# Gate and up of the half steps by a block algorithm with seven products for eight, with the output product in thirds and a list-scheduled order

## The chip, the cores and the metric

The kernel runs on one core of a Trainium2 chip. The time is the device time of one execution in microseconds; lower is better. The engines are TensorE (PE: matmuls, with its weight loads shown apart as PEld), VectorE (DVE), ScalarE (ACT), GpSimd (POOL) and SyncE (SP, which issues the DMAs here).

## What is computed

A decoder trunk of two layers on 512 tokens of width 1024 in float32. Each layer is a half step, a mixer and a second half step; the change is in the four half steps:

```python
def swiglu(x, wi, wo):
    gate, up = jnp.split(x @ wi, 2, axis=-1)
    return (jax.nn.silu(gate) * up) @ wo
...
        h = h + 0.5 * swiglu(rms_norm(h, ffn1_norm[li]), ffn1_wi[li], ffn1_wo[li])
        hn = rms_norm(h, mix_norm[li])
...
        h = h + mix
        h = h + 0.5 * swiglu(rms_norm(h, ffn2_norm[li]), ffn2_wi[li], ffn2_wo[li])
```

`wi` is 1024 x 5632 (gate and up, 2816 features each), `wo` is 2816 x 1024. The mixer of layer 0 is gated linear attention beside causal pooling (`gla_pool_mixer`), that of layer 1 sparse attention with an indexer that chooses 128 keys (`dsa_mixer`); a final norm ends the trunk.

## The kernel before

All activations lie transposed in SBUF: `h` is eight tiles of 128 features x 512 tokens. A float32 product is made of three passes of PE: every operand is kept as a high and a low part (`hi` + `lo`), and `mm3` (L152 to L156) issues high x high, high x low, low x high. The high part is a ScalarE copy to float32r, the low part a VectorE subtraction. `post` (L215) makes these parts of `h` times the norm's gain, `hgh0..7` and `hgl0..7`. The norm's factor `R` (one number per token) is multiplied in afterwards.

Weights come as chunks of 128 x 2048 in the order of their use. `w_load` issues the DMA into one of two raw tiles `wr`, `w_split` (L121) makes `wh` (L144) and `wl` (L145) of the whole chunk and then loads the chunk after the next; `w_get` hands out the parts. Each of `wr`, `wh` and `wl` has two buffers.

A half step, `ffn` (L250), goes through the 22 feature blocks in two halves of 11. For a block it runs 8 tiles x gate and up x 3 passes = 48 matmuls of 512 columns into two PSUM banks. `evac` (L253) makes the activation: gate times `R` (L255), silu (L256), up times `R` (L258), their product (L259), high part `acth` (L262) and low part `actl` (L263). After eleven blocks the output product adds 8 tiles `m` of 11 blocks, each 33 matmuls of 512 columns into one bank (`out_block`, L308), and L327 adds half the bank to `h[m]`. In the second half of a half step `post` and `squares` prepare the next norm. The last half step makes its two last output tiles in pieces of 256 tokens, so that the norm and the stores of the first 256 lie beside the products of the second (`piece`, `final`).

Instructions go to each engine in the order in which the program calls them, written out by hand: `w_split` and `bg_step` after each block (the latter runs steps of the rotary tables in the second half step). Engines wait on each other through semaphores. The mixers use the same stream of weights: `proj` (L377) for projections of 512 columns, `v_mm` (L535) and `v_tile` for values, with the weights as the moving operand on 256 columns, `eo_pool` (L793) and `oo` (L1080) for their output products.

SBUF tiles are laid out pool after pool and, inside a pool, in order of first use, each padded to a multiple of 32 bytes; pools stand in the order `const`, `wpool`, `hgpool`, `small`, then the pool of the stage at hand.

## Time and profile before

| | us |
|---|---|
| median of 3 runs | 1850.26 |
| lowest, highest | 1849.87, 1858.63 |
| span of the profiled execution | 1855.0 |
| busy in it: PE, PEld, VectorE, ScalarE, GpSimd | 1834.0, 1494.0, 887.9, 599.6, 195.7 |

The span runs from the first to the last instruction of the one profiled execution. A matmul's listed duration overlaps the next one's, so the step from one start to the next is what it costs; the busy time of PE is the union of all of them. A row's last part, in brackets or behind a bar, is the idle time of the engine before it and what ended it.

### The profile page before, as it was taken

What the parts mean: (1) busy time and instruction counts of PE and PEld (TensorE: products, weight loads), DVE (VectorE), ACT (ScalarE), POOL (GpSimd) and SP (SyncE); (2) the same over time, 40 slices, a digit from 0 to 9 for tenths busy, and PEclk for the clock granted to TensorE, in tenths of its full rate; (3) what the DMA queues carried; (4) which work ended last, traced back from release to release, by engine and by line L of the source; (5) the groups of instructions that cost most, each with busy time, mean ns of one, the idle gap of its engine ahead of it and who ended that gap; (6) DMA issues with size and microseconds to landing.
All of it is one profiled execution on the core that took longest, in us unless ns stands there. A gap on an engine that the chain in (4) does not pass through costs nothing.

```text
span 1855.0 us, 19748 instructions
## 1 busy us (share of the span) xinstructions
PE 1834.0 (99%) x8330; PEld 1494.0 (81%) x8330; DVE 887.9 (48%) x1144; ACT 599.6 (32%) x717; POOL 195.7 (11%) x159
## 2 busy tenths in 40 slices
PE   9999999999999999999999999999999999999997
PEld 6888888888678888888888888888687888888886
DVE  6442444348455552444344424444797444334443
ACT  5321223243253322223333212233346432212232
POOL 0000000134320000000100000001475200000002
PEclk9999999999899999999999999999999999999999
DMA  5222222131112232222232222222121122222221
GB/s 184 91 102 91 93 111 92 62 126 69 46 69 97 93 111 81 101 104 91 79 114 91 101 93 91 98 107 82 60 92 46 69 91 99 105 99 93 92 91 57
DMA packets 28361, 169.97 MB, mean 92 GB/s; under 512 B 3152, under 2 KB 6128, under 8 KB 9072
## 3 DMA queue, kind: packets, MB, share of 16 engines
q1 hardware_dynamic: 28272, 168.71, 25.0%
q8 instruction: 65, 1.06, 0.2%
q14 instruction: 24, 0.20, 0.0%
HBM read 166.60 MB, written 2.10 MB: 91 GB/s over the span
## 4 chain that ended last, share of the span: by engine, by line
PE 92%; DVE 4%; issue 1%; ACT 1%; POOL 1%; DMA 0%; SPq 0%; DVEq 0%; ACTq 0%; POOLq 0%
PE o L155 9%; PE o L154 9%; PE o L156 9%; PE g L156 9%; PE u L156 9%; PE u L154 9%; PE u L155 9%; PE g L154 9%; PE g L155 9%; PE pj L154 2%; PE pj L155 1%; PE pj L156 1%; PE oo L155 1%; PE oo L154 1%; PE oo L156 1%
## 5 line engine op out<-in xcount | busy, mean ns | idle before, releaser
L145 DVE TENSOR_TENSOR wl<-wr,wh 128x2048 fp32r<-128x2048 f32 (+3 forms) x151 | 323.6, 2144 | 299.5 <-ACT wh L144 298.8
L144 ACT ACTIVATE wh<-wr 128x2048 fp32r<-128x2048 f32 (+3 forms) x166 | 298.1, 1797 | 249.1 <-PE o L155 179.7
L154 PE MATMUL o<-acth,wh 128*128 128x512 f32 (+1 forms) x726 | 281.3, 387 | 0.0
L155 PE MATMUL o<-actl,wh 128*128 128x512 f32 (+1 forms) x726 | 281.1, 387 | 0.0
L156 PE MATMUL o<-acth,wl 128*128 128x512 f32 (+1 forms) x726 | 281.1, 387 | 0.0
L154 PE MATMUL g<-hgh_f,wh 128*128 128x512 f32 x704 | 275.8, 392 | 1.7 <-ACT wh L144 1.7
L154 PE MATMUL u<-hgh_f,wh 128*128 128x512 f32 x704 | 274.5, 390 | 0.0
L156 PE MATMUL g<-hgh_f,wl 128*128 128x512 f32 x704 | 274.4, 390 | 0.1
L155 PE MATMUL g<-hgl_f,wh 128*128 128x512 f32 x704 | 274.3, 390 | 0.0
L155 PE MATMUL u<-hgl_f,wh 128*128 128x512 f32 x704 | 274.1, 389 | 0.0
L156 PE MATMUL u<-hgh_f,wl 128*128 128x512 f32 x704 | 274.0, 389 | 0.0
L230 POOL TENSOR_TENSOR acc<-acc,sq 128x512 f32<-128x512 f32 x35 | 53.1, 1518 | 1482.7 <-ACT sq L229 1482.7
L258 DVE TENSOR_TENSOR u<-u,R 128x512 f32<-128x512 f32 x88 | 60.7, 690 | 300.6 <-PE u L156 300.6
L262 ACT ACTIVATE acth<-u 128x512 fp32r<-128x512 f32 x88 | 55.6, 632 | 373.2 <-DVE u L259 373.2
L154 PEld LDWEIGHTS o<-acth,wh 128*128 128x128 f32 x726 | 136.0, 187 | 31.6
L155 PEld LDWEIGHTS o<-actl,wh 128*128 128x128 f32 x726 | 135.9, 187 | 31.5
L156 PEld LDWEIGHTS o<-acth,wl 128*128 128x128 f32 x726 | 135.9, 187 | 31.3
L154 PEld LDWEIGHTS g<-hgh_f,wh 128*128 128x128 f32 x704 | 132.2, 188 | 32.1 <-ACT wh L144 4.1
L155 PEld LDWEIGHTS g<-hgl_f,wh 128*128 128x128 f32 x704 | 132.4, 188 | 28.7 <-issue 0.7
L156 PEld LDWEIGHTS g<-hgh_f,wl 128*128 128x128 f32 x704 | 132.2, 188 | 28.0 <-DVE wl L145 0.6
L155 PEld LDWEIGHTS u<-hgl_f,wh 128*128 128x128 f32 x704 | 132.2, 188 | 27.8 <-issue 0.2
L156 PEld LDWEIGHTS u<-hgh_f,wl 128*128 128x128 f32 x704 | 132.3, 188 | 27.6
(286 smaller groups left out, 2070.1 us busy)
## 6 DMA issues: line engine op xcount, KB each, us to landing
wr<-in_wi_dram SPq DMA_DIRECT2D x87, 1024.0 KB, 4.8
wr<-in_wo_dram SPq DMA_DIRECT2D x40, 1024.0 KB, 4.8
wr<-in_wev_dram SPq DMA_DIRECT2D x8, 1024.0 KB, 4.8
wr<-in_wod_dram SPq DMA_DIRECT2D x7, 1024.0 KB, 4.8
wr<-in_wo_dram SPq DMA_DIRECT2D x8, 512.0 KB, 3.7
wr<-in_wevo_dram SPq DMA_DIRECT2D x4, 1024.0 KB, 4.8
wr<-in_wodo_dram SPq DMA_DIRECT2D x4, 1024.0 KB, 4.8
h<-in_xT_dram SPq DMA_DIRECT2D x8, 256.0 KB, 6.2
```

Of the source, the lines that this page charges most:

```text
L144: A.activation(hi[:, p0:p1], raw[:, p0:p1], AF.Copy)
L145: eng.tensor_tensor(lo[:, p0:p1], raw[:, p0:p1], hi[:, p0:p1], op=ALU.subtract)
L154: T.matmul(ps, st[0], mv[0], start=start, stop=False)
L155: T.matmul(ps, st[0], mv[1], start=False, stop=False)
L156: T.matmul(ps, st[1], mv[0], start=False, stop=stop)
L230: (eng or G).tensor_tensor(acc[:, a:b], acc[:, a:b], sq[:, a:b], op=ALU.add)
L258: V.tensor_tensor(u1, up, R, op=ALU.mult)
L262: A.activation(hi, u1, AF.Copy)
```

## The change

Gate and up of feature blocks 3 to 21 are computed by a block algorithm on 2 x 2 blocks: of the weights, gate and up by the first and second half of the 1024 inputs; of the activations, the first and second half of the inputs by the first and second half of the tokens. Seven products of 128 x 512 by 512 x 256 take the place of eight, and sums of blocks are formed before and after them:

- Of each weight chunk (`"S"`, stored as four blocks of 512 columns and loaded by two DMAs) VectorE forms four sums (`outer`, one operation of 1024 columns, and two of 512). `split_part` makes high and low parts of three stretches, `ab` (1024 columns, unit 0), `ds` (1536, unit 2 or 3 in turn) and `z` (1024, unit 1). The units hold the parts in single buffers.
- Of the activations `add_blocks` forms four sums per pair of tiles once in a half step: `TH` and `TL`, in 4 tiles of 1024 columns each.
- `seven_products` runs 7 products of 4 tiles x 3 passes of 256 columns into two banks, `A_` and `BC`. ScalarE copies partial sums out of them (`s1`, `s5`, `s2`, `t4`), VectorE adds (`gate`, `u3`). Products seven and four of a block run between the first products of the next one, or inside the first output tile. Up is no longer multiplied by `R`; the output is (`scaled`, two VectorE operations per tile instead of one).

Blocks 0 to 2 (`PLAIN`) stay as they were. The output product is made after 8, 7 and 7 blocks (`THIRDS`) instead of after 11 and 11, so `h[m]` is added to three times. A half step is first built as a list of tasks with durations and dependences (`Schedule`), and then issued in the order in which a list schedule of these tasks on the engines starts them; PE's order and the DMA queue's are kept as they are written.

Tiles move: `hgpool` stands before `wpool`, small tiles named `shift` are put in, weight units begin at an offset (`off`, in words of 4 bytes) by the kind of use, a 4-byte tile goes out of the pool of the rotary tables, and the scratch space at the bottom shrinks from 16384 to 1024 bytes. Four tiles of the first mixer and six of the second move into the tails of the raw tiles. The last products of the second mixer run as two of 256 columns instead of one of 512. The core of the diff:

```diff
+THIRDS = ((0, 8), (8, 15), (15, 22))
+PLAIN = (0, 1, 2)
+UNIT = 1024
+UPAD = 64
...
+        while any(queues.values()):
+            best = None
+            for eng, q in queues.items():
+                for t in q[:1] if eng in ("PE", "SP") else q:
+                    if all(d.end is not None for d in t.deps):
+                        ready = max([clock[eng]] + [d.end + (self.LAG if d.eng != eng else 0.0) for d in t.deps])
+                        key = (ready, t.late, t.n)
+                        if best is None or key < best[0]:
+                            best = (key, t)
+            (start, _, _), t = best
+            t.end = clock[t.eng] = start + t.dur
+            queues[t.eng].remove(t)
+            done.append(t)
+        for t in done:
+            t.fn()
+        return clock
...
+    def chunk(kind, src, n, eng=V, units=(0, 1), off=0):
+        chunks.append((kind, src, n, eng, units, off))
     def ffn_chunks(i):
-        for half in range(2):
-            chunks.extend((wi[i, half * HF + f], V) for f in range(HF))
-            chunks.extend((wo[i, half, c, :, 0:min(16, KD * HF - 16 * c) * P], V) for c in range(6))
+        for t, (fa, fb) in enumerate(THIRDS):
+            for f in range(fa, fb):
+                if f in PLAIN:
+                    chunk("P", wi[i, f], 2048, units=(2, 3) if f == 1 else (0, 1), off=48)
+                else:
+                    chunk("S", wi[i, f], 2048)
+            for m in range(0, KD, 3):
+                n = (fb - fa) * P
+                c0 = fa * KD * P + m * n
+                chunk("O", wo[i, :, c0:c0 + min(3, KD - m) * n], min(3, KD - m) * n)
...
+    srcs = [wpool.tile([P, 3584], F32, name=f"src{n}") for n in range(2)]
+    wa_sb = wpool.tile([P, KD * 2 * RANK], F32R, name="wa_sb")
+    wpool.tile([P, 16], F32, name="shift")
...
+    def unit_tile(u, off, name):
+        n = (UNIT if u < 2 else UNIT + S) + UPAD
+        return tuple(wpool.tile([P, n], F32R, tag=f"u{u}{x}", name=f"u{x}_{name}")[:, off:n] for x in "hl")
...
+            nc.sync.dma_start(srcs[c % 2][:, 512:1536], src[:, 0:1024])
+            nc.sync.dma_start(srcs[c % 2][:, 2560:3584], src[:, 1024:2048])
+        else:
+            nc.sync.dma_start(srcs[c % 2][:, 0:n], src)
...
+            def split_part(c, u, held, a, n, *deps):
+                raw = srcs[c % 2][:, a:a + n]
+                def hi():
+                    held[:] = [x[:, 0:n] for x in unit_tile(u, 0, f"{c}_{a}")]
+                    A.activation(held[0], raw, AF.Copy)
+                th = add("ACT", act_us(n), hi, deps, readers[u])
+                tl = add("DVE", dve_us(n), lambda: V.tensor_tensor(held[1], raw, held[0], op=ALU.subtract), th)
+                readers[u] = []
+                src_free[c % 2].extend((th, tl))
+                return tl
...
+            TH = [fp.tile([P, 1024], F32R, tag=f"th{k}", name=f"th{k}") for k in range(4)]
+            TL = [fp.tile([P, 1024], F32R, tag=f"tl{k}", name=f"tl{k}") for k in range(4)]
+            fp.tile([P, 16], F32, name="shift")
...
+            def seven_products(f, t, c, parts_, tls, before):
+                A_, BC = new_bank("a"), new_bank("bc")
+                d = {"third": t}
+                (ab, z, ds), (t_ab, t_z, t_ds) = parts_, tls
+                def product(rec, half, st, j, mv, start, stop, *deps):
+                    u, pair = st
+                    def mms():
+                        for k in range(4):
+                            mm3(ps_of(rec)[:, half * 256:half * 256 + 256], col(tuple(pair), j * S + k * P, j * S + (k + 1) * P),
+                                mv(k), start and k == 0, stop and k == 3, not start)
+                    tp = add("PE", 12 * 0.1134, mms, deps)
+                    readers[u].append(tp)
+                    return tp
+                def x_(tile_, half):
+                    return lambda k: tuple(x[:, half * 256:half * 256 + 256] for x in hg[k + tile_])
+                def t_(n):
+                    return lambda k: (TH[k][:, n * 256:n * 256 + 256], TL[k][:, n * 256:n * 256 + 256])
...
+                p1 = product(A_, 0, ab, 0, x_(0, 0), True, True, t_ab, A_["after"])
+                s1 = add("ACT", a_, snap("p1", lambda: d["sp"][:, 0:256], lambda: ps_of(A_)[:, 0:256]), p1,
+                         after_ring(sp_ring, 2))
+                if before:
+                    before.pop(0)()
+                p2 = product(BC, 0, ab, 1, x_(4, 0), True, True, t_ab, BC["after"])
+                p5 = product(BC, 1, ds, 1, t_(0), True, True, t_ds, blocks, p2)
+                s5 = add("ACT", a_, snap("p5", lambda: d["p5"], lambda: ps_of(BC)[:, 256:512]), p5,
+                         after_ring(p5_ring, 2))
+                if before:
+                    before.pop(0)()
+                p6 = product(A_, 0, z, 0, t_(2), False, True, t_z, s1)
+                s2 = add("ACT", a_, snap("u2", lambda: d["sp"][:, 256:512], lambda: ps_of(A_)[:, 0:256]), p6)
+                p3 = product(BC, 1, z, 1, x_(4, 1), False, True, s5)
+                def gate():
+                    d["g"] = ft.tile([P, S], F32, tag="g", name=f"g{f}")
+                    V.tensor_tensor(d["g"], ps_of(BC), d["sp"], op=ALU.add)
+                t1 = add("DVE", dve_us(S) + 0.06, gate, p3, s2, g_ring[-2:-1])
+                sp_ring.append(t1)
+                BC["free"].append(t1)
+                t2 = add("DVE", dve_us(S), lambda: V.tensor_tensor(d["g"], d["g"], R, op=ALU.mult), t1)
+                t3 = add("ACT", act_us(S), lambda: A.activation(d["g"], d["g"], AF.Silu), t2)
+                silus.append(t3)
+                def seven():
+                    p7 = product(A_, 0, ds, 2, t_(1), False, True, s2)
+                    def u3():
+                        d["up"] = ft.tile([P, S], F32, tag="up", name=f"up{f}")
+                        V.scalar_tensor_tensor(d["up"][:, 256:512], ps_of(A_)[:, 0:256], -1.0, d["p5"], op0=ALU.mult,
+                                               op1=ALU.subtract)
+                    d["u3"] = add("DVE", v + 0.03, u3, p7, s5, after_ring(up_ring, 2))
+                    p5_ring.append(d["u3"])
+                def four():
+                    p4 = product(A_, 0, ds, 0, t_(3), False, True, d["u3"])
+                    t4 = add("ACT", a_, lambda: A.activation(d["up"][:, 0:256], ps_of(A_)[:, 0:256], AF.Copy, scale=-1.0),
+                             p4)
+                    A_["free"].append(t4)
+                    t5 = add("DVE", dve_us(S), lambda: V.tensor_tensor(d["g"], d["g"], d["up"], op=ALU.mult), t3, t4)
+                    up_ring.append(t5)
+                    act_out(f, d, t5)
+                return [seven, four]
...
+            def seven_split(c, f):
+                src = srcs[c % 2]
+                load_up_to(c)
+                def outer():
+                    cc = src[:, 512:1024]
+                    V.tensor_tensor(src[:, 1536:2560].rearrange("p (s c) -> p s c", s=2),
+                                    src.rearrange("p (s c) -> p s c", c=S)[:, 2:6:3], cc[:, None, :].to_broadcast([P, 2, S]),
+                                    op=ALU.add)
+                ab, z, ds = [], [], []
+                ga = 2 + (at["ds"] % 2)
+                at["ds"] += 1
+                t_ab = split_part(c, 0, ab, 2560, 1024, loaded.get(c))
+                t0 = add("DVE", dve_us(1024), outer, loaded.get(c))
+                t_ds = split_part(c, ga, ds, 1024, 1536, t0)
+                t1 = add("DVE", dve_us(S), lambda: V.tensor_tensor(src[:, 0:512], src[:, 1536:2048], src[:, 2560:3072],
+                                                                   op=ALU.add), t0)
+                t2 = add("DVE", dve_us(S), lambda: V.tensor_tensor(src[:, 512:1024], src[:, 0:512], src[:, 3072:3584],
+                                                                   op=ALU.add), t1)
+                t_z = split_part(c, 1, z, 0, 1024, t2)
+                load_up_to(c + 2)
+                return ((0, ab), (1, z), (ga, ds)), (t_ab, t_z, t_ds)
...
+            def out_split(m, nb, c):
+                load_up_to(c)
+                u = m % 4
+                held = wo_parts[m] = []
+                wo_tl[m] = split_part(c, u, held, (m % 3) * nb * P, nb * P, loaded.get(c))
...
+            def scaled(m, ps, a=0, b=S):
+                x = ft.tile([P, S], F32, tag="up", name=f"o{m}")
+                V.scalar_tensor_tensor(x[:, a:b], ps[:, a:b], 0.5, R[:, a:b], op0=ALU.mult, op1=ALU.mult)
+                V.tensor_tensor(h[m][:, a:b], h[m][:, a:b], x[:, a:b], op=ALU.add)
...
+                        continue
+                    rec = new_bank("o")
+                    if m == 0:
+                        tp = out_task(rec, m, t, 0, 3)
+                        if pending:
+                            pending.pop(0)()
+                        tp = out_task(rec, m, t, 3, nb - 3 if pending else nb - 1)
+                        if pending:
+                            pending.pop(0)()
+                            tp = out_task(rec, m, t, nb - 3, nb - 1)
+                        held_back = rec
+                        if rope_steps and t < 2:
+                            dep = tp
+                            for fn in rope_steps["ia"[t]]:
+                                dep = add("DVE", 1.0, fn, dep)
+                        continue
+                    if m == 1:
+                        tp = out_task(rec, m, t, 0, nb - 1)
+                        out_end(held_back, 0, t, out_task(held_back, 0, t, nb - 1, nb))
+                        tp = out_task(rec, m, t, nb - 1, nb)
+                    else:
+                        tp = out_task(rec, m, t, 0, nb)
+                    out_end(rec, m, t, tp)
...
+            heads2 = ev.tile([P, 2], F32, name="heads2")
+            ev.tile([P, 40], F32, name="shift")
...
                         (ovh[k // 4][:, k % 4, a:b_], ovl[k // 4][:, k % 4, a:b_]), k == 0, k == KD - 1)
@@ -1101,7 +1606,7 @@
...
-                    oo(m, 0, 512)
+                    oo(m, 0, 256)
```

## Rows read from the trace of the kernel before

**Rows 1.** page, busy time by engine, and the chain that ended last by engine.

```profile
PE 1834.0 (99%) x8330; PEld 1494.0 (81%) x8330; DVE 887.9 (48%) x1144; ACT 599.6 (32%) x717; POOL 195.7 (11%) x159
...
PE 92%; DVE 4%; issue 1%; ACT 1%; POOL 1%; DMA 0%; SPq 0%; DVEq 0%; ACTq 0%; POOLq 0%
```

**Rows 2.** stretches: gate and up, output, first mixer, second mixer; columns named first.

```profile
core 0: us, PE busy (x) PEld busy (x) DVE busy (x) ACT busy (x) POOL busy (x), PEclk, DMA share, GB/s
...
191.60:311.20 119.60, 119.60 (x529) 99.04 (x528) 53.37 (x53) 33.17 (x32) 0.00 (x0) 1.00 0.28 105
311.20:372.80 61.60, 61.60 (x265) 49.30 (x265) 23.69 (x23) 19.64 (x23) 7.78 (x6) 1.00 0.21 77
372.80:564.40 191.60, 189.53 (x957) 149.62 (x956) 109.37 (x148) 76.34 (x100) 68.61 (x58) 0.96 0.21 76
...
1291.40:1479.70 188.30, 182.66 (x953) 148.92 (x952) 137.68 (x340) 88.90 (x171) 91.88 (x64) 0.98 0.21 74
```

**Rows 3.** PE's timeline, gate and up; columns: start, duration, line, tiles, shape, count.

```profile
47.67 0.39 PE L154 MATMUL g<-hgh_f,wh 128*128 128x512 f32 x1
...
53.11 0.39 PE L154 MATMUL u<-hgh_f,wh 128*128 128x512 f32 x1
```

**Rows 4.** PE's timeline, output product of the last half step, 512 columns.

```profile
1822.20 0.39 PE L154 MATMUL o<-acth,wh 128*128 128x512 f32 x1
...
1827.10 0.39 PE L154 MATMUL o<-acth,wh 128*128 128x512 f32 x1
```

**Rows 5.** PE's timeline, the last output pieces, 256 columns.

```profile
1828.15 0.28 PE L154 MATMUL o<-acth,wh 128*128 128x256 f32 x1
...
1834.61 0.28 PE L154 MATMUL o<-acth,wh 128*128 128x256 f32 x1
```

**Rows 6.** PE's timeline, values of the first mixer, 256 columns.

```profile
402.68 0.28 PE L154 MATMUL v<-wh,hgh_mix 128*128 128x256 f32 x1
...
414.56 0.28 PE L154 MATMUL v<-wh,hgh_mix 128*128 128x256 f32 x1
```

**Rows 7.** VectorE's groups by form; columns as in part 5 of the page.

```profile
L145 DVE TENSOR_TENSOR wl<-wr,wh 128x2048 fp32r<-128x2048 f32 x133 | 304.9, 2293 | 251.3 <-ACT wh L144 250.7 <-POOL isc L1097 0.6
...
L258 DVE TENSOR_TENSOR u<-u,R 128x512 f32<-128x512 f32 x88 | 60.7, 690 | 300.6 <-PE u L156 300.6
...
L145 DVE TENSOR_TENSOR wl<-wr,wh 128x1024 fp32r<-128x1024 f32 x13 | 15.8, 1224 | 48.2 <-ACT wh L144 48.2
...
L1088 DVE TENSOR_TENSOR h<-oo,h 128x256 f32<-128x256 f32 x8 | 3.4, 420 | 4.4 <-PE oo L156 4.4
```

**Rows 8.** VectorE's timeline, one gate-and-up block, and later a back-to-back pair.

```profile
239.28 2.29 DVE L145 TENSOR_TENSOR wl<-wr,wh 128x2048 fp32r<-128x2048 f32 x1 [1.11 <-ACT wh L144]
241.49 0.68 DVE L255 TENSOR_TENSOR g<-g,R 128x512 f32<-128x512 f32 x1
246.17 0.69 DVE L258 TENSOR_TENSOR u<-u,R 128x512 f32<-128x512 f32 x1 [4.00 <-PE u L156]
246.96 0.69 DVE L259 TENSOR_TENSOR u<-g,u 128x512 f32<-128x512 f32 x1
...
584.83 0.68 DVE L255 TENSOR_TENSOR g<-g,R 128x512 f32<-128x512 f32 x1
585.43 0.68 DVE L258 TENSOR_TENSOR u<-u,R 128x512 f32<-128x512 f32 x1
```

**Rows 9.** ScalarE's groups by form.

```profile
L144 ACT ACTIVATE wh<-wr 128x2048 fp32r<-128x2048 f32 x148 | 281.9, 1905 | 198.0 <-PE o L155 129.8 <-issue 53.0 <-PE pj L155 15.1
...
L256 ACT ACTIVATE g<-g 128x512 f32<-128x512 f32 x88 | 55.6, 632 | 265.9 <-DVE g L255 265.9
...
L144 ACT ACTIVATE wh<-wr 128x1024 fp32r<-128x1024 f32 x13 | 13.5, 1054 | 51.1 <-PE o L155 49.9 <-DMA wr<-in_wi_dram 1.2
...
L544 ACT ACTIVATE v_sb<-v,rcol 128x256 f32<-128x256 f32 x8 | 3.4, 469 | 2.9 <-PE v L156 2.8
```

**Rows 10.** timeline of the last piece: its last matmul, VectorE's first operation.

```profile
1843.54 0.28 PE L156 MATMUL o<-acth,wl 128*128 128x256 f32 x1
...
1844.17 0.41 DVE L351 SCALAR_TENSOR_TENSOR h<-o,h 128x256 f32<-128x256 f32 x1
```

**Rows 11.** page, DMA issues: weights, KB each, us from issue to landing.

```profile
wr<-in_wi_dram SPq DMA_DIRECT2D x87, 1024.0 KB, 4.8
...
wr<-in_wo_dram SPq DMA_DIRECT2D x8, 512.0 KB, 3.7
```

More of the change, by code (lines that the diff above doesn't have):

```diff
@@ new lines, in split_small, with split_hi @@
+    def split_small(c):
+        both = wa_sb.rearrange("p (k s c) -> p k s c", s=2, c=RANK)
+        x = srcs[c % 2][:, 0:KD * RANK].rearrange("p (k c) -> p k c", c=RANK)
+        A.activation(both[:, :, 0], x, AF.Copy)
+        V.tensor_tensor(both[:, :, 1], x, both[:, :, 0], op=ALU.subtract)
+        parts[c] = wa_sb
+    def split_hi(c, n):
+        kind, src, cols, eng, units, off = chunks[c]
+        hi, lo = unit_tile(units[n], off, f"{c}_{n}")
+        parts.setdefault(c, []).append((hi, lo))
+        w = min(UNIT, cols - n * UNIT)
+        A.activation(hi[:, 0:w], srcs[c % 2][:, n * UNIT:n * UNIT + w], AF.Copy)
```

605 lines of the change are left out of this document (417 added, 188 removed).

## The prediction

> **What bounds the kernel now.** I read the page first: TensorE is busy for 1834.0 of 1855.0 us and carries 92% of the chain that ended last; VectorE is busy 48% of the span, ScalarE 32% [rows 1]. The table of stretches says the same of each stage: in the gate and up products and in the output product of a half step PE never pauses, at the full granted clock, and only the two mixers leave it some idle time [rows 2]. So time comes off where PE gets fewer columns or a shorter step per column, and goes back on where a new wait stops PE.
>
> A matmul's listed duration is a modelled latency, so I take the step from start to start. Four steps matter. Gate and up, 512 columns: 24 steps from 47.67 to 53.11 us, 226.7 ns each [rows 3]. Output product, 512 columns: 21 steps in 4.90 us, 233.3 ns [rows 4]. Output product on 256 columns: 57 steps in 6.46 us, 113.3 ns [rows 5]. Values of the first mixer, 256 columns: 99 steps in 11.88 us, 120.0 ns [rows 6]. The shape does not decide between the two steps of one width; the tiles do. Adding up tile sizes in order of allocation (each padded to 32 bytes), all weight tiles and hgh/hgl start 96 bytes past a multiple of 128, acth/actl start at 32 (64 in the second half step). So at 512 columns moving and stationary tile at the same offset gave 226.7, at another 233.3; at 256 columns the same offset gave 120.0 and offsets 64 bytes apart gave 113.3.
>
> **Gate and up by seven products.** One block was 8 tiles x 2 x 3 = 48 matmuls of 512: 48 x 226.7 = 10.88 us. It becomes 7 products x 4 tiles x 3 = 84 matmuls of 256. The new order of pools (two raw tiles of 14336 bytes, wa_sb, then 64 bytes named shift) puts the weight units at 32, while hg stays at 96 and TH/TL, first in their pool, come to 96: 64 apart. That pair was seen only the other way round (moving 32, stationary 96), so the step is bounded by 113.3 and 120.0 [rows 5, 6]; I take 113.3: 84 x 113.3 = 9.52 us. Saved: 1.36 us x 19 blocks x 4 half steps = 103.4 us (at 120.0: 0.80 x 76 = 60.8). The three plain blocks put their weights 192 bytes further (off=48), at 96 as hg: 226.7 as now, no change.
>
> **Output product.** Its 528 tile products a half step stay. The second 64 bytes named shift put acth/actl at 32, as the units: same offset, so I take 226.7 for 233.3 (bounds: these two). Now there are 2046 matmuls of 512 and, in the last half step, 132 of 256: 2046 x 233.3 + 132 x 113.3 ns = 492.4 us. With thirds the last pieces are fewer, 84, and at one offset: 2070 x 226.7 + 84 x 120.0 = 479.3 us. Saved 13.1 us.
>
> A page of the Trainium skill speaks against both address terms: "SBUF — State Buffer", section "Who interferes with whom", gives PE two independent read ports, one for the moving operand and one for weights, and says that PE waits on nobody. By that rule where a tile lies changes no step; rows of one shape here differ by 6.7 ns [rows 3, 4], so the trace does not agree, and the case in which addresses do nothing is the second rival.
>
> **Mixers.** Value products (288 matmuls) get offsets 64 apart: 288 x 6.67 = 1.9 us; the two output products and the probabilities' product get a little. I take 2.5 us, bounds 0 and 5. Splitting the last odd-mixer products into two halves of 256 moves no columns.
>
> **What the other engines must do for one of the 76 blocks.** VectorE has eleven operations: three low parts (1024, 1536, 1024), the double sum (1024), two sums (512 each), gate sum, product with R, gate times up and the activation's low part (512 each), and u3 (256). Durations: 1024 1.224, 512 0.69, 256 0.42, 1536 between the rows of 1024 and 2048, 1.76 [rows 7]. Back to back, the next operation starts 0.08 us before the listed end (241.49 - 239.28 = 2.21 for 2.29; 0.60 for 0.68), and 0.10 after it where it reads the one before (246.17, 246.96) [rows 8]. The sum is 3 x 1.14 + 1.67 + 6 x 0.60 + 0.33 = 9.0 us at best, 10.0 by listed durations, 11.1 with a hop after each. PE's block is 9.52. ScalarE: 2 x 1.05 + 1.48 for the high parts, 4 x 0.47 for copies out of PSUM, 2 x 0.63: 6.7 us [rows 9], not near. VectorE comes from 4.9 us of 10.88 (53.37 over 11 blocks [rows 2]) to the edge of being the bound. What saves it: of a third's seven blocks the first one's weight work (6.3 us) is done during the output product before it, so 7 x 9.0 - 6.3 = 57 us stand against 66.6 of PE; and in the output product VectorE has 8 x (1.0 + 1.5) = 20 us of work in 38.
>
> **New waits on PE.** Units 0 and 1 are single: unit 0 is free after the second product and wanted by the next block's first, 4 products = 5.44 us later; the chain is 0.52 (a matmul's slot end to VectorE's start: 1843.54 + 0.11 to 1844.17 [rows 10]) + 1.05 + 0.1 + 1.22 + 0.1 = 3.0 us, so VectorE may be 2.4 late. Unit 1 has 6.8 us. The third's last block has a shorter cover: between its seventh product and its fourth lie only 3 matmuls of 512 (0.68 us; 6 in the first third), while u3 needs 0.52 + 0.42 + 0.1 = 1.04 and perhaps 0.6 for the operation in front: about 0.9 x 8 + 0.2 x 4 = 8 us. The second third begins with the unit (3) that the last output tile still reads: 0.52 + 1.48 + 0.1 + 1.76 + 0.1 = 3.96 against two products, 2.72: 1.2 x 4 = 5 us. Inside the runs I allow 0.05 us a block, 4 us. Together 17 us, bounds 0 and 40 (0.35 a block instead). The waiting matmul holds all of PE behind it, since PE's order is fixed.
>
> **What is free and what covers it.** The bytes loaded stay the same; a block's 1 MB lands in 4.8 us (two of 512 KB, 3.7 each) [rows 11] and a raw tile comes round every 2 x 9.52 us, of which its weight work takes 6.3 us of VectorE and 3.6 of ScalarE; without that room each block would wait for the rest of its 4.8 us. SP issues one more DMA per block and more at the end. The tables of the rotary angles, the extra two VectorE operations per output tile and TH/TL (4 x (4 x 0.42 + 2 x 0.7) = 12 us on VectorE in the 32.6 us of the plain blocks) lie beside PE; if VectorE lags there, the first block pays it, up to 4 us a half step. At the very end the output gets one more operation of 256 in the chain: + 0.5 us.
>
> **The sum.** 1855.0 - 103.4 - 13.1 - 2.5 + 0.5 + 17 = 1753.5 us of span. The median of the runs, 1850.26, lies 4.7 us under that profiled span; so 1748.8, say 1749.
>
> **Rivals.** (1) VectorE becomes the bound of the runs: a block takes 10.0 to 11.1 us, + 0.5 to 1.6 x 76 = 36 to 120 us on the sum without waits (1731.8): 1768 to 1852, 1800 a little under the middle. For it: 9.0 of 9.52 already at best; against it the work done ahead. (2) Addresses do nothing, or the mirrored pair takes the longer step: the products keep 120.0, the output 233.3: 1855.0 - 60.8 + 0.5 + 9 - 4.7 = 1799 (at 113.3, 1764). For it: two pairs are all the evidence. (3) On the other side, slower: VectorE's queue is in order and its list is fixed, so u3 and the gate sum stand at its head until their product ends, with split work behind them, and PE and VectorE take turns. Each of the two can hold it for one product, 1.36 us: 9.0 + 2.7 = 11.7 us a block, + 0.84 x 76 = 64, less 15 for the other parts: 1899. It costs time from 2.1 us of such idling a block on. Against it: the list puts other work first wherever that work is ready.
>
> **How the numbers follow.** Forecast 1749, chance 0.66, own range 1728 to 1768 (no waits and mixers at 5; waits at 35). Rival 1: 0.19; rival 2: 0.11; rival 3: 0.04. Low end 1728; high end 1800, which takes in half of rival 1 and rival 2 at 120. About 0.5% is what a measurement of this kernel can tell from no change: rival 1's upper end and a part of rival 3 give 0.02 for the same, 0.04 slower, 0.94 faster.
>
> **What would show it.** Right: in a run of seven blocks PE starts every 113.3 ns with 84 matmuls per block, output steps are 226.7, the gate-and-up stretches shrink by 1.36 us per block, and PE's idle time is in pieces of about 1 us at the start of each output product and of each second third. Wrong: steps of 120 or 233.3 (rival 2); VectorE busy above 95% in the runs and PE idle before products on VectorE's low parts (rival 1), or PE and VectorE both well under 90% busy there (rival 3). The step of 256 columns and VectorE's nearness to the bound are what could make it wrong.

## The result, and the profile after

| | median | lowest to highest | runs | profiled span |
|---|---|---|---|---|
| before | 1850.75 us | 1849.87 to 1858.63 | 4 | 1855.0 us |
| after | 1795.09 us | 1791.95 to 1801.09 | 4 | 1793.3 us |

The ratio is 0.9695, with a 95% interval of 0.967 to 0.972. The forecast was 1749 us, with a range of its own up to 1768 and a whole range up to 1800. The time lies in the whole range, but 46 us above the forecast and outside the forecast's own range. One term of the sum, the output product, came about as it was written; the rest of this document is about the 46 us.

The page of after, busy time by engine, one group of VectorE and the chain that ended last by engine, beside [rows 1]:

```profile
PE 1743.9 (97%) x11138; PEld 1559.7 (87%) x11138; DVE 1369.5 (76%) x1882; ACT 861.6 (48%) x1301; POOL 196.4 (11%) x175
...
PE 83%; DVE 9%; issue 2%; DMA 2%; ACT 2%; POOL 1%; SPq 0%; DVEq 0%; ACTq 0%; POOLq 0%
...
L670 DVE TENSOR_TENSOR src<-src 128x1024 f32<-128x1024 f32 x76 | 92.8, 1222 | 38.9 <-DMA src<-in_wi_dram 38.9
```

PE is still the bound, but it is idle for 49 us where it was idle for 21, and in the chain VectorE's share rose from 4 to 9% and DMA's from 0 to 2%. The last line is the double sum of the seven-product blocks: VectorE stood idle 38.9 us in front of it, waiting for the weights' DMA.

The stretches of after, beside [rows 2]: a run of seven blocks, the output product behind it, the first mixer, the second mixer.

```profile
core 0: us, PE busy (x) PEld busy (x) DVE busy (x) ACT busy (x) POOL busy (x), PEclk, DMA share, GB/s
254.90:321.00 66.10, 66.10 (x563) 66.10 (x562) 56.11 (x65) 38.54 (x58) 0.00 (x0) 1.00 0.36 121
321.00:362.20 41.20, 41.20 (x197) 34.41 (x196) 31.33 (x37) 20.16 (x29) 7.92 (x6) 1.00 0.29 101
362.20:549.40 187.20, 185.35 (x958) 147.30 (x957) 113.03 (x152) 75.86 (x110) 69.98 (x66) 0.97 0.22 72
1238.80:1433.40 194.60, 184.16 (x1049) 154.82 (x1048) 137.54 (x348) 88.80 (x181) 89.89 (x71) 0.97 0.19 66
```

Inside a run of seven blocks PE never waits (66.10 of 66.10), and VectorE is busy 85% of the time. So neither VectorE's load (rival 1) nor its order (rival 3) stops PE there. The weight loader (PEld) has no gap either: in products of 256 columns it is as busy as PE, in the output product, at 512, it is not (34.41 of 41.20). The second mixer is longer than before, 194.6 us for 188.3.

The output product, PE's timeline of after in the last half step, beside [rows 4]:

```profile
1744.64 0.39 PE L274 MATMUL o<-acth,uh 128*128 128x512 f32 x1
...
1750.31 0.39 PE L275 MATMUL o<-actl,uh 128*128 128x512 f32 x1
```

25 steps in 5.67 us are 226.8 ns, where before took 233.3. Over all 2070 such matmuls the mean is 226.9 ns, and the 84 pieces of 256 columns take 120: this term came as forecast.

The seven products have **two steps**. Two stretches of 20 us that hold nothing but them, in the second half step (columns as in the stretches above):

```profile
610.00:630.00 20.00, 20.00 (x172) 20.00 (x171) 18.39 (x23) 12.12 (x18) 0.00 (x0) 1.00 0.39 132
690.00:710.00 20.00, 20.00 (x179) 20.00 (x178) 16.33 (x20) 11.79 (x18) 0.00 (x0) 1.00 0.40 136
```

172 matmuls in one and 179 in the other (both counts take in some two that stick out at the ends) are steps of 117.8 and 113.3 ns. Operands, offsets and the granted clock are alike. Of the 6384 steps 38% took about 113.3 and most of the others about 117.8; what exceeds 113.3 in the steps without a wait sums to 17.4 us. From one block to the next the step stays as it is: in this execution it changed only where PE had paused or had done output products, and a run entered from output products without a pause was always at 117.8.

The waits of PE, whole span of after (us in total, times, longest):

```profile
PE a L274 <- ACT uh L432: 10.8, 3, 7.1
PE a L276 <- DVE ul L434: 9.1, 4, 2.6
PE oo L274 <- DVE h L1593: 6.1, 4, 2.8
```

The first two lines all stand at one place: the first seven-product block behind the plain blocks, once in each half step. In the second half step, VectorE's timeline (start, duration, in brackets the idle time in front and what ended it) and then PE's:

```profile
554.33 0.69 DVE L361 TENSOR_TENSOR acc<-acc,sq 128x512 f32<-128x512 f32 x1
560.22 1.23 DVE L670 TENSOR_TENSOR src<-src 128x1024 f32<-128x1024 f32 x1 [5.21 <-DMA src<-in_wi_dram]
561.36 0.48 DVE L491 SCALAR_TENSOR_TENSOR tsa<-h,cs,b 128x256 f32<-128x256 f32 x1
```

```profile
582.74 0.39 PE L276 MATMUL u<-hgh_f,ul 128*128 128x512 f32 x1
585.29 0.38 PE L274 MATMUL a<-hgh_f,uh 128*128 128x256 f32 x1 [2.16 <-ACT uh L432]
585.51 0.28 PE L275 MATMUL a<-hgl_f,uh 128*128 128x256 f32 x1
588.40 0.58 PE L276 MATMUL a<-hgh_f,ul 128*128 128x256 f32 x1 [2.62 <-DVE ul L434]
588.78 0.42 PE L274 MATMUL a<-hgh_f,uh 128*128 128x256 f32 x1
589.00 0.42 PE L275 MATMUL a<-hgl_f,uh 128*128 128x256 f32 x1
```

VectorE has the T sums (`TH` and `TL`) and the plain blocks to do (from 561.36 on), but its list begins with the double sum of block 3, whose weights land at 560.2. It stands there for 5.21 us; PE pays 24 us later, 2.16 and 2.62 us. Then PE's steps are 0.21 us instead of 0.113: the granted clock was 0.5 (1.2 instead of 2.4 GHz) for 6.8 us from 587.2 on. Against its usual steps PE loses 7.9 us here, 4.8 of them in the two waits.

The third line of the waits is in the second mixer, PE's timeline and VectorE's:

```profile
1404.22 0.28 PE L276 MATMUL oo<-oTh,ul 128*128 128x256 f32 x1
1407.29 0.58 PE L274 MATMUL oo<-oTh,uh 128*128 128x256 f32 x1 [2.79 <-DVE h L1593]
1407.67 0.42 PE L275 MATMUL oo<-oTl,uh 128*128 128x256 f32 x1
```

```profile
1404.54 2.36 DVE L243 TENSOR_TENSOR ul<-src,uh 128x1024 fp32r<-128x1024 f32 x2 [0.19 <-ACT uh L237]
1406.82 0.42 DVE L1593 TENSOR_TENSOR h<-oo,h 128x256 f32<-128x256 f32 x1
```

An output tile's second half of 256 columns goes into the bank of its first half (`pso[m, 0]` in the code) and waits until VectorE has added the first half to `h`. That addition stands behind two low parts of the next weights in VectorE's list. Here too half clock follows (steps of 0.21 us).

### The profile page after: what moved, and what is told of

The parts are those of the page before. It is cut to its first block, busy times and chain, and to the rows that moved or that the text cites. A ratio compares the mean times of both kernels' runs of the same rounds, so it can differ in the third digit from the quotient of the medians.

```text
span 1793.3 us, 27209 instructions
## 1 busy us (share of the span) xinstructions
PE 1743.9 (97%) x11138; PEld 1559.7 (87%) x11138; DVE 1369.5 (76%) x1882; ACT 861.6 (48%) x1301; POOL 196.4 (11%) x175
## 4 chain that ended last, share of the span: by engine, by line
PE 83%; DVE 9%; issue 2%; DMA 2%; ACT 2%; POOL 1%; SPq 0%; DVEq 0%; ACTq 0%; POOLq 0%
PE o L276 9%; PE o L274 9%; PE o L275 9%; PE a L276 8%; PE a L274 8%; PE a L275 8%; PE bc L276 6%; PE bc L274 6%; PE bc L275 6%; DMA src<-in_wi_dram 2%; PE pj L274 2%; PE pj L276 2%; PE pj L275 2%; DVE ul L243 1%; DVE ul L434 1%
## 5 line engine op out<-in xcount | busy, mean ns | idle before, releaser
L432 ACT ACTIVATE uh<-src 128x1024 fp32r<-128x1024 f32 (+2 forms) x324 | 367.5, 1140 | 463.7 <-PE o L275 232.7
L434 DVE TENSOR_TENSOR ul<-src,uh 128x1024 fp32r<-128x1024 f32 (+2 forms) x324 | 426.0, 1320 | 39.2 <-ACT uh L432 33.5
L274 PE MATMUL o<-acth,uh 128*128 128x512 f32 (+1 forms) x718 | 276.6, 385 | 0.0
L275 PE MATMUL o<-actl,uh 128*128 128x512 f32 (+1 forms) x718 | 276.4, 385 | 0.0
L276 PE MATMUL o<-acth,ul 128*128 128x512 f32 (+1 forms) x718 | 276.4, 385 | 0.0
L274 PE MATMUL a<-th,uh 128*128 128x256 f32 x912 | 255.4, 280 | 0.0
L275 PE MATMUL a<-tl,uh 128*128 128x256 f32 x912 | 254.6, 279 | 0.0
L276 PE MATMUL a<-th,ul 128*128 128x256 f32 x912 | 254.5, 279 | 0.0
L276 PEld LDWEIGHTS a<-th,ul 128*128 128x128 f32 x912 | 173.4, 190 | 0.0
L275 PEld LDWEIGHTS a<-tl,uh 128*128 128x128 f32 x912 | 171.4, 188 | 0.6
L670 DVE TENSOR_TENSOR src<-src 128x1024 f32<-128x1024 f32 x76 | 92.8, 1222 | 38.9 <-DMA src<-in_wi_dram 38.9
```

The source lines that it names most:

```text
L274: T.matmul(ps, st[0], mv[0], start=start, stop=False, skip_group_check=on)
L275: T.matmul(ps, st[0], mv[1], start=False, stop=False, skip_group_check=on)
L276: T.matmul(ps, st[1], mv[0], start=False, stop=stop, skip_group_check=on)
L432: A.activation(held[0], raw, AF.Copy)
L434: tl = add("DVE", dve_us(n), lambda: V.tensor_tensor(held[1], raw, held[0], op=ALU.subtract), th)
L670: V.tensor_tensor(src[:, 1536:2560].rearrange("p (s c) -> p s c", s=2), src.rearrange("p (s c) -> p s c", c=S)[:, 2:6:3], cc[:, None, :].t ...
```

## Experiments

All are the changed kernel with the edit shown, unless said otherwise. Their times go against 1795.1 us; before took 1850.2 to 1852.0 us beside all but the last, where it took 1856.9.

**The halves in the second mixer.**

```diff
-                if m < 4:
-                    oo(m, 256, 512)
-                else:
-                    oo(m, 0, 256)
-                    oo(m, 256, 512)
+                oo(m, 256 if m < 4 else 0, 512)
```

> The last four output tiles of the odd mixer again as one product of 512 columns each, in a bank of its own; all else as in the changed kernel. Theory A: the changed kernel's odd mixer (194.6 us against 188.3 before) is longer because the second half of a tile is written to the bank that VectorE still reads for the first half: PE waits 6.1 us at four places there (longest 2.79) and then runs 256-column steps of 213 ns at half clock for 3.4 us and more. Whole products take both away: 1795.1 - 6.1 - about 2 of half clock = 1787, 1784 to 1790. Theory B: the waits are for VectorE's own lag in the mixer and come back at other matmuls there: 1794 to 1797. The output matmuls at 512 columns take 227 ns by the tiles' places (moving 96, stationary 32) or, with these places unequal, 233: 96 x 6.7 = 0.6 us, beside the point.

Measured: 1782.4 us (1781.4 to 1785.6), 12.7 less. The waits on `h` are gone, and the second mixer's stretch (columns as above) is 9.6 us shorter:

```profile
1233.70:1418.70 185.00, 180.63 (x955) 147.66 (x953) 136.82 (x344) 88.80 (x181) 89.91 (x71) 0.99 0.20 70
```

The cause is settled. The other 3 us lie outside the stretch that was edited: 53% of the 256-column steps were at 113.3 in this run's profile, where after had 38%, and what exceeds 113.3 is 4.2 us less.

**What VectorE's list begins with.**

```diff
+            if i > 0:
+                for c, us in ((at["use"] + 2, 2.0), (at["use"] + 3, 9.0)):
+                    loaded[c] = add("SP", us, lambda: None)
```

> In the second, third and fourth half step the list scheduler is told that the two raw tiles asked for before the half step are there only 2 and 11 us after its start (it took them as there at once). VectorE's double sum for the first seven-product block then goes behind the sums for T and the plain blocks' work instead of heading VectorE's list. Theory A: the head of the list that waits for its DMA (VectorE idle 5.21 us before 560.22, 3.99 before 904.78, 4.60 before 1443.35) is what makes PE late at the first seven-product block: the waits of 5.4, 2.5 and 4.8 us there go, and half of the 10.2 us at half clock behind them: 1795.1 - 12.7 - 5 = 1777, 1774 to 1785. Theory B: VectorE has too much work in the plain blocks whatever its order (TH and TL alone are 12 us), and the waits stay within 2 us: 1791 to 1797. The first half step, where no DMA headed the list, does not change in either.

Measured: 1779.1 us (1771.9 to 1783.9), 16.0 less. VectorE's timeline at the same place, and PE's waits over the whole span:

```profile
546.86 0.69 DVE L361 TENSOR_TENSOR acc<-acc,sq 128x512 f32<-128x512 f32 x1
547.47 0.48 DVE L491 SCALAR_TENSOR_TENSOR tsa<-h,cs,b 128x256 f32<-128x256 f32 x1
...
556.32 1.22 DVE L670 TENSOR_TENSOR src<-src 128x1024 f32<-128x1024 f32 x1
```

```profile
PE a L274 <- ACT uh L432: 6.7, 1, 6.7
PE a L276 <- DVE ul L434: 1.6, 1, 1.6
```

The T sums come at once, the double sum follows 9 us later without a wait, and of seven waits two are left, both in the first half step, which the edit does not touch. Theory A holds: not VectorE's load but its list, made by a scheduler that took two raw tiles as there, cost the three later half steps their waits. No work was taken away.

**The worth of the seven products alone**, in two runs: all 22 blocks by eight products (`PLAIN = tuple(range(22))`, their weight units in turn, no T sums), with the halves in the second mixer and with whole products there.

> All 22 feature blocks by eight products (48 matmuls of 512 columns each, 10.88 us); no T sums; the output product in thirds, the schedule and the tiles' places as in the changed kernel. This gives the worth of the seven products alone, with what they cost at their edges. Theory A (the accounting of the two traces): 76 blocks give 103.4 us at a step of 113.3 ns, 17.4 of them are lost to steps of 117.8, about 28 to waits and half clock at the first such block of each half step: about 52 net, so 1795 + 48 to 58 = 1843 to 1853 minus what before's own profiled run lay above its median (about 6): 1837 to 1850, steps of 226.7 ns in all of gate, up and output. Theory B: the seven products do not pay at all and the whole gain is the output product and the schedule: below 1800.

> All 22 blocks by eight products, and the last four output tiles of the odd mixer as whole products: what is left of the change is the output product in thirds, the schedule and the tiles' places. With the halves it took 1850.7 us, as long as the kernel before. Theory A: the output product's 13.4 us and the mixers' few are there, and the halves in the odd mixer ate them (6.3 us of waits there, the rest half clock): 1850.7 - 12.7 = 1838, 1835 to 1841. Theory B: the halves cost only their 6.3 us of waits, since in this kernel no half clock follows elsewhere, and the rest is lost in the new schedule: 1843 to 1846.

Measured: 1850.7 us (1847.3 to 1854.7, 10 runs; ratio to before 0.9995, interval 0.9983 to 1.0007) and 1837.5 us (1837.2 to 1843.6; ratio 0.9913, interval 0.9882 to 0.9944). In the first of them PE's longest sum of waits is the halves':

```profile
PE oo L274 <- DVE h L1593: 6.3, 4, 3.1
```

The steps of the output product are 226.9 ns there too, but the halves in the second mixer ate the whole gain; without them it shows. With whole products in both, the seven products are worth 1837.5 - 1782.4 = 55.1 us with all that they cost at their edges, where the sum had 103.4 - 17 = 86.4.

**The tiles' places.**

```diff
-                    held[:] = [x[:, 0:n] for x in unit_tile(u, 0, f"{c}_{a}")]
+                    held[:] = [x[:, 0:n] for x in unit_tile(u, 48, f"{c}_{a}")]
```

> The weight units of the seven products and of the output product lie 192 bytes further on, so that stationary operands lie at 96 modulo 128 bytes instead of 32; every instruction and its place in the order stay. Theory A, from pairs of places in the two traces: 256 columns take 120.0 ns where moving and stationary lie equal modulo 128, 113.3 or 117.8 where they lie 64 apart; 512 columns the other way, 226.7 equal and 233.3 apart. The seven products go from 113.3/117.8 (mean about 116.0) to 120.0 throughout: 6384 x 4.0 = +25.5 us; the output product from 226.7 to 233.3: 2070 x 6.6 = +13.7; its last 84 pieces of 256 from 120 to 113.3: -0.6. Time 1795 + 38.6 = 1834, 1828 to 1840. Theory B: where a tile lies changes no step, and another cause made the output product faster: 1792 to 1798.

Measured: 1829.5 us (1828.5 to 1832.2), 34.4 more, where A said 38.6 and B none. PE's timeline, seven products and then output steps:

```profile
709.36 0.28 PE L274 MATMUL a<-hgh_f,uh 128*128 128x256 f32 x1
...
711.76 0.28 PE L276 MATMUL a<-th,ul 128*128 128x256 f32 x1
...
1770.55 0.40 PE L274 MATMUL o<-acth,uh 128*128 128x512 f32 x1
...
1772.41 0.40 PE L276 MATMUL o<-acth,ul 128*128 128x512 f32 x1
```

20 steps in 2.40 us are 120.0 ns, now without a second value; 8 steps in 1.86 us are 232.5, and the mean over 2070 output matmuls is 233.4. Instructions and their order are the same, so where the tiles lie is alone the cause, and rival 2 falls. The page "SBUF — State Buffer" of the Trainium skill says in "Who interferes with whom" that PE never waits on anyone. Read as the prediction read it, as a rule on where tiles lie, it would have left this run no slower; it took 34.4 us more.

**VectorE's room inside a run.**

```diff
-                    V.tensor_tensor(src[:, 1536:2560]...
+                    for _ in range(2):
+                        V.tensor_tensor(src[:, 1536:2560]...
```

> The changed kernel with the double sum of each seven-product block executed twice on VectorE (1.14 us more in each of 76 blocks, planned for in the schedule); the results are the same. Theory A: inside the runs VectorE has room: 56.1 us busy in 66.1 us of seven blocks, so 8.0 us more fit without a wait of PE (64.1 of 66.1), and only the first such block of each half step gets later, by one or two of these sums and some half clock: 1800 to 1812. Theory B (the first rival of the prediction: VectorE at 10 to 11 us a block is the bound or just under it, with the hops between dependent operations): each block gets up to 1.1 us longer: 1840 to 1880.

Measured: one run, 1798.0 us, 2.9 more. In the same stretch VectorE is now busy 59.12 us; PE's waits, whole span:

```profile
254.90:321.00 66.10, 66.03 (x560) 65.82 (x560) 59.12 (x67) 35.79 (x54) 0.00 (x0) 1.00 0.34 118
```

```profile
PE a L274 <- ACT uh L432: 18.8, 4, 7.1
PE a L276 <- DVE ul L434: 6.4, 4, 2.8
```

Five of the run's seven double sums lie in this stretch, in both kernels, and the list moved other work out of it, so 3.0 us came on top here and not 8.0; VectorE is then busy 89% of the time. 76 times 1.14 us more on VectorE cost PE next to nothing in the runs and 5.3 us more of waits at the edges (25.2 for 19.9). VectorE was not the bound of the runs, up to this load. (A larger share of steps at 113.3, 53%, hid some 4 us of it.)

**What sets the step of 256 columns.** A short matmul into the unused half of a bank, ahead of three of four blocks:

```diff
+                        if start and rec is A_ and f % 4:
+                            n_ = f % 4 * 64
+                            T.matmul(ps_of(rec)[:, 256:256 + n_], pair[0][:, 0:P], mv(0)[0][:, 0:n_], start=True,
+                                     stop=True, skip_group_check=True)
```

> The changed kernel with one extra matmul of 64, 128 or 192 columns (by the block's number; every fourth block gets none) into an unused half of the bank, ahead of the first product of a seven-product block; the results are the same. Each costs about one step, 57 x 0.115 = 6.6 us. The question is the step of the 256-column products, 113.3 in some runs of blocks and 117.8 in others at the same places of the tiles. Theory A: the step is set by how the weight loads fall against the matmuls, and keeps only while the stream is regular: at blocks with an extra short matmul it changes between the two values, at blocks without one it never does. Theory B: it belongs to the place in the program (banks, buffers, what the DMAs do then): the runs at 113.3 and 117.8 stand where they stood in the changed kernel. Time by A 1795 + 6.6, give or take 17 by the share of the two steps; by B 1802.

Measured: one run, 1792.7 us. PE's timeline at a short matmul of 64 columns and at one of 192:

```profile
685.41 0.28 PE L276 MATMUL bc<-hgh_f,ul 128*128 128x256 f32 x1
685.52 0.19 PE L596 MATMUL a<-hgh_f,uh 128*128 128x64 f32 x1
685.55 0.36 PE L274 MATMUL a<-hgh_f,uh 128*128 128x256 f32 x1
685.75 0.28 PE L275 MATMUL a<-hgl_f,uh 128*128 128x256 f32 x1
...
686.93 0.28 PE L276 MATMUL a<-hgh_f,ul 128*128 128x256 f32 x1
```

```profile
705.18 0.25 PE L596 MATMUL a<-hgh_f,uh 128*128 128x192 f32 x1
705.27 0.30 PE L274 MATMUL a<-hgh_f,uh 128*128 128x256 f32 x1
705.41 0.28 PE L275 MATMUL a<-hgl_f,uh 128*128 128x256 f32 x1
```

The step before 685.52 is 113.3, the ten from 685.75 to 686.93 are 118. Of 36 short matmuls of 64 or 128 columns inside runs, all 36 turned the step (20 from 113.3 to 117.8, 16 back); of 12 with 192 columns none did. At the four third thirds, which are entered straight from output products, 192 columns led to 113.3 (the next expectations say 5 of 5; the trace has four such places). Blocks without one changed only where the stream was broken: at the pauses of the second thirds, and once, at 932.9 us, at a single step of 217 ns. So the step belongs to how the stream stands at a moment, not to the place in the program, as theory A had it, with a rule that it did not have (64 and 128 turn, 192 does not). That weight loads set it, as theory A also says, no run shows.

**Using it**, first with both repairs alone and then with twelve short matmuls, one ahead of the first product of each run, and `at["ds"] = 0` at each third's start (with this reset the second thirds begin with a unit that the last output tile does not read):

> Whole products in the odd mixer and the raw tiles' arrival told to the scheduler, nothing else. Theory A: the two causes lie in different stages and add: 1795.1 - 12.7 - 16.0 = 1766.4, 1762 to 1770. Theory B: the half clock after the waits is shared between them (the two medians moved by more than the waits that went, 6.1 and 12.7 us), and a part of it comes back elsewhere: 1770 to 1775.

> Both repairs; besides, one short matmul of 192 columns ahead of the first product of each run of seven-product blocks (12 in all, 1.4 us), and the unit of the differences (U2 or U3) is chosen anew at each third's start, so that the second third's first block no longer wants the unit that the last output tile still reads (0.31 us of pause, four times). The run with short matmuls at three of four blocks had these regularities: 64 or 128 columns turned the step from 113.3 to 117.8 or back at 36 of 36 places, 192 columns left it at 12 of 12 inside a run, and 192 columns behind output products led to 113.3 at 5 of 5 places, where no short matmul always led to 117.8. Theory A: the step of a whole run is set by this phase at its entry, so that with 192 columns and no pause nearly all runs stay at 113.3: of 16.9 us that the steps of 117.8 cost some 14 go: 1766.4 - 14 + 1.4 - 1.2 = 1753, 1749 to 1757. Theory B: the regularities were those of one execution, and the step is drawn anew: 1763 to 1770.

> As the run with 192 columns, but the twelve short matmuls have 64 columns; the same number of instructions, and no more columns. Theory A: since 64 columns turn the step where 192 leave it, runs entered from output products go to 117.8: 12 to 15 us longer than with 192 columns, 1764 to 1770. Theory B: any short matmul does the same, or none does anything, and the two runs agree within 3 us.

Measured: 1768.6 us (1767.8 to 1771.4) with both repairs, 1750.8 (1750.2 to 1758.0) with 192 columns, 1749.3 (1748.3 to 1751.8; ratio to before 0.9451, interval 0.9433 to 0.9469) with 64. A stretch of 20 us of seven products with the repairs alone and one with 192 columns:

```profile
800.00:820.00 20.00, 20.00 (x172) 20.00 (x171) 19.90 (x25) 12.16 (x18) 0.00 (x0) 1.00 0.31 107
```

```profile
690.00:710.00 20.00, 20.00 (x179) 20.00 (x178) 18.51 (x23) 13.12 (x20) 0.00 (x0) 1.00 0.35 106
```

The repairs add. With 192 columns 96% of the steps are at 113.3 (26% with the repairs alone), and what exceeds 113.3 falls from 20.8 us to 1.2; the time falls by 17.8. The expectation for 64 columns was wrong: they too led to 113.3, at 11 of the 11 entries without a wait, so at the entry of a run either width does it, and the turning rule holds inside runs only. The reset did not run alone, but it changes nothing at the first and third thirds: there the entries without a wait went to 117.8 at 7 of 7 places with the repairs alone and to 113.3 at 14 of 14 with a short matmul (two runs), so the short matmul is the cause there; at the second thirds the two are not separated. Why a short matmul decides it was not found. These two runs do not differ beyond their spread, and both are faster than before and after.

**The first half step**, with a fourth block by eight products there, once with the repairs and once with the short matmuls as well. In the first of these two runs block 3's weights kept the layout for seven products, so its output is another one; order and times of the work are not touched by that.

> Both repairs together (whole products in the odd mixer, worth 12.7 us alone; the raw tiles' arrival told to the scheduler, worth 16.0 alone) and one more: in the first half step alone a fourth block is computed by eight products, so that its first seven-product block comes 10.9 us later. Without the third repair the two would add to 1795.1 - 28.7 = 1766.4. Theory A: in the first half step VectorE is simply busy without a gap from 18 to 60 us (squares, the norm, T sums, two weight blocks), and PE waits 6.7 and 1.6 us at the first seven-product block and runs at half clock behind; one more plain block gives VectorE 10.9 us, of which it needs 2.5, so waits of about 8 us and some 5 us of half clock go, for the 1.0 to 1.4 us that a seventh product saves in one block: 1766.4 - 11.5 = 1755, 1752 to 1759. Theory B: the wait there is not for VectorE's load but for something fixed to the first seven-product block (its chunk's DMA, the T sums' chain), and moves with it: 1764 to 1768.

> As the run with short matmuls of 64 columns, and in the first half step a fourth block by eight products, so that the run begins at block 4 there. Theory A: PE's waits at that edge (6.6 us for a high part, 1.4 for a low part) shrink to the 4.9 us that the earlier run with a fourth block showed, and the 10.2 us at half clock to 6.8: -3.1 - 1.7 + 1.4 for the block = -3.4: 1749.3 - 3.4 = 1746, 1743 to 1748. Theory B: the fourth block only moves the wait to the next block's weights: 1749 to 1752.

Measured: 1766.1 us (1762.4 to 1771.4), against 1768.6 without the fourth block, and 1753.2 (1749.9 to 1756.3; ratio to before 0.9453), against 1749.3 (0.9451). No gain is shown. PE's waits at the edge became smaller in the traces (6.4 and 1.6 us with the repairs alone, then 2.2, 1.0 and 0.8 in the first run; 3.3, 2.2 and 1.3 in the second) and moved to the new first block and the next one. Theory A had them too small: about 8 us were to go in the first run and 4.9 to be left in the second, where 4 and 6.8 were left. What feeds the first block there, VectorE's load, its list or ScalarE's, stays open.

## Why the prediction was right or wrong

The sum had six terms. Each beside what the traces show, in us:

| term | in the sum | measured | from |
|---|---|---|---|
| steps of the seven products | -103.4 | -86.0 | 17.4 over 113.3 |
| output product | -13.1 | -12.4 | sums of its steps, 492.6 and 480.2 |
| mixers | -2.5 | +1.9 | first mixer 191.6 to 187.2, second 188.3 to 194.6 |
| end of the span | +0.5 | +3.0 | start of the last output matmul to the end, 11.5 and 14.5 |
| new waits, with half clock behind them | +17 | +31.3 | steps longer than usual, gate and up: 37.2, before 6.0 |
| profiled execution to median | -4.7 | +1.8 | time and span of after |

By the measured column 1855.0 becomes 1792.8 us of span; 1793.3 were measured. That the whole range held the time is luck: its upper end came from rivals 1 and 2, and the prediction's own range ends at 1768. (The lower end of that range, with no waits and the mixers at 5, works out at 1729, not 1728; nothing hangs on it.)

**Right: the output product and the places of the tiles.** 226.8 ns for [rows 4]'s 233.3; moving the units by 192 bytes gave the old step back. The two pairs of rows on which the rule rested were enough.

**Mis-sized: 113.3 for the seven products.** The step that failed is "I take 113.3", with 120.0 as the only other value. The mirrored pair has two steps, 113.3 and 117.8, and 38% of the matmuls got the first. [Rows 5] came from one uninterrupted stretch and could show only one value; the values of [rows 6] had another pair of places. The price was 17.4 us, and the runs with short matmuls gave it back.

**Wrong place: the waits.** The sum put 8 us between the seventh and the fourth product at the thirds' ends; there single steps are 0.1 to 0.3 us longer, under 2 us in all. It put 5 us at the second thirds' starts; 0.3 each came. It put 4 us inside the runs; none came. Instead 28 us stand at the first seven-product block of the four half steps, 19.9 of them waits, most of the others half clock. The prediction named that place ("if VectorE lags there, the first block pays it, up to 4 us a half step") and left it out of the sum, and it asked only how much VectorE has to do in the plain blocks (12 us in 32.6), not what stands at the head of its list when the half step begins. The run with the arrival times shows that the list was the cause in three of the four half steps. Half clock, which came with three of these four edges, was not in the price either.

**Wrong sign: the mixers.** The step that failed is "splitting the last odd-mixer products into two halves of 256 moves no columns". True, and it cost 9.6 us against whole products: the second half was given its first half's bank, which VectorE frees only after what stands before it in its queue. A new reader-before-writer dependence is a new wait on PE, and it had to be looked for in the diff like the others. In the first mixer 4.4 us went, but up to 3.4 of them by the clock, which was at 0.5 for 17.1 us there in before's profile and for 10.2 in after's; most of the value products' steps came to 118, not to 113.3.

**Mis-sized: the end of the span.** The step that failed is "the output gets one more operation of 256 in the chain: + 0.5 us". In before VectorE starts on the last output 0.63 us after the last matmul's start [rows 10]. After, PE's last output matmul and VectorE:

```profile
1778.81 0.28 PE L276 MATMUL o<-acth,ul 128*128 128x256 f32 x1
1779.07 2.49 DVE L856 TENSOR_TENSOR y<-y,R 128x256 f32<-128x256 f32 x4
1781.48 0.41 DVE L712 SCALAR_TENSOR_TENSOR o<-o,R 128x256 f32<-128x256 f32 x1
```

Now it is 2.67 us: four operations for the first half's output stand in front of it in VectorE's list, as at the other two places. The operation that was added, and PE's sums for the norm at half clock, are the last 1 us. No run changed this.

**Wrong: -4.7 from span to median.** The profiled execution of before was longer than its median because its granted clock was lower: 0.992, where eleven others of that kernel, recorded beside the first experiments with spans of 1846.8 to 1852.0, had 0.993 to 0.997. Such long executions come up again later (0.991 and 0.992 with spans of 1854.9 to 1857.9), and which kind was profiled is chance. In [rows 2] the first mixer has PEclk 0.96, and a sum made against it should have set half clock aside stage by stage.

**The rivals.** Rival 1 held the measured time in its range, for another reason: inside the runs VectorE was not the bound, and 1.14 us more a block did no harm there. What the prediction reckoned for VectorE there, 57 us in 66.6, came: 56.1 in 66.1. Rivals 2 and 3 fall by the run with the units moved and by PE's 66.10 of 66.10; of rival 2 a part came, since the mirrored pair did take a longer step, 117.8, in most places. What the seven products can give was about as forecast: with both repairs and the short matmuls the kernel takes 1749.3 us, 88.2 less than with eight products throughout, where the sum had -103.4 + 17 = -86.4. That it meets the forecast of 1749 is partly luck, since the terms are not the same.

## What to carry to other kernels

When a change makes an engine's list from a schedule, read what each engine has at the head of its list at every edge between stages, and check that what the schedule takes as there at time zero is there. The same holds for the last operations of the span. A product that is cut in two needs a second bank or a reader that is next in its queue; else the cut is a wait (neither was run here; the product was left whole). Where a step was read in one uninterrupted stretch, bound it by the nearest other step seen at the same shape, and do not take that one stretch for the rule.

## What was not expected of the hardware

- The same 256-column matmuls with the same tiles go at 113.3 or 117.8 ns and keep the one they have until the stream is broken. Behind a pause either came; a short matmul of 64 or 128 columns turned it (36 of 36), one of 192 left it (12 of 12), and either 64 or 192 ahead of a run led to 113.3 (22 of 22 entries without a wait in two runs, at the second thirds together with the other unit order).
- By the tiles' places, added up from their sizes: with moving and stationary operand equal modulo 128 bytes, 256 columns took 120.0 ns and 512 took 226.8; 64 bytes apart, 113.3 or 117.8 and 233.4. What is better for one width is worse for the other. At 256 columns the weight loader has no gap (66.10 of 66.10 us), at 512 it has (34.41 of 41.20). The page "TensorE: Matmul & The Clock Gate" of the Trainium skill, section "Back-to-back issue gap", says that in a stream of load and matmul pairs both set the spacing. The loader without a gap fits that, but 113.3 is also half of 226.8, as columns alone would give it, so no run here shows which of the two sets the step.
- At three of the four edges PE's granted clock fell to 0.5, for 3.4 to 10.2 us at a time, and so waits of 4.2, 4.8 and 8.7 us in sum cost 6.0, 7.9 and 11.5. In the third half step, with one wait of 2.2 us, it did not fall.
